# Log-softmax over rows of 50,000: two DMA queues and a register-counted loop over four 50 KB buffers

## The chip, the cores and the metric

The kernel runs on one NeuronCore of one Trainium2 chip. The metric is the device time of the whole program in microseconds (us). Before the change the median of 17 runs is 7909.7 us (7871.91 to 7929.28).

The names of the profile: PE is TensorE (matmul), PEld its weight load, DVE is VectorE, ACT is ScalarE, POOL is GpSimd and SP is SyncE, which here only issues transfers. "SPq" is SP's queue of instructions.

## The reference

The input has 16 x 512 = 8192 rows of 50,000 float32 numbers, 1638.4 MB. The output has the same shape. For each row:

```python
max_x = np.max(x, axis=-1, keepdims=True)
shifted = x - max_x
log_sum_exp = np.log(np.sum(np.exp(shifted), axis=-1, keepdims=True))
return (shifted - log_sum_exp).astype(np.float32)
```

Each number is read once and written once, so at least 3276.8 MB cross between HBM and the on-chip memory.

## The kernel before, in words

A row is cut into G = 8 pieces of 6,250 numbers, and each piece lies on its own partition. A tile has 16 rows, that is 128 partitions of 25,000 bytes, 3.2 MB; there are 512 tiles. Eight buffers hold tiles. Everything is unrolled in Python, and the order within each engine is the order in which the code is written (`manual_schedule`); engines wait for each other only through semaphores where data or buffers require it.

Three functions make up the work on a tile:

- `load(t)` issues the transfer of tile t on SP (L75).
- `front(t)`: VectorE takes the maximum of each partition (L81). A transpose (L84), a reduction over the 8 partitions of a row (L86), a copy that spreads the result (L91) and a second transpose (L96) give every partition the negative maximum of its row, `negmax`. ScalarE then takes the exponential of the tile in two pieces of 3,125, with the sum as a by-product in `part` (L102); the exponentials themselves go to a dump in PSUM and are not used. TensorE multiplies the two sums with a block matrix of ones, which adds them over the partitions of a row (L108), and ScalarE takes the logarithm (L112).
- `back(t)`: VectorE subtracts maximum and logarithm in place (L117), and SP issues the store of the tile (L121).

The main loop (L125 to L131) runs, for each t: load of tile t+5, front of tile t, back of tile t-1. So on VectorE the maximum of tile t is taken before tile t-1 is subtracted, and on SP loads and stores alternate in one queue. The load of tile t+5 goes into the buffer that tile t-3 had, so SP waits for the store of tile t-3 before it issues that load, and the store of tile t-1 stands behind it in SP's order.

Of the kernel before, what the change touches and what calls it, by code (L numbers as in the profile page):

```python
# [1 line left out]

# [4 lines left out]


FP32 = mybir.dt.float32
ACT = mybir.ActivationFunctionType  # L10
ALU = mybir.AluOpType
AX = mybir.AxisListType.X

P = 128
SQ = 32

G = 8
R = P // G
EXP_C = 3125
NBUF = 8  # L20
AHEAD = 5


@with_exitstack
def kernel(
    ctx: ExitStack,
    tc: tile.TileContext,
    x: bass.AP,
    out: bass.AP,
):  # L30
    nc = tc.nc
    xf = x.flatten_outer_dims()
    of = out.flatten_outer_dims()
    N, V = xf.shape
    W = V // G
    assert N % R == 0 and V % G == 0 and W % EXP_C == 0
    ntiles = N // R
    nexp = W // EXP_C

    xt = xf.rearrange("(t r) (g w) -> t (r g) w", r=R, g=G)  # L40
    ot = of.rearrange("(t r) (g w) -> t (r g) w", r=R, g=G)

    data = ctx.enter_context(tc.tile_pool(name="data", bufs=NBUF))
    stats = ctx.enter_context(tc.tile_pool(name="stats", bufs=4))
    consts = ctx.enter_context(tc.tile_pool(name="consts", bufs=1))
    dump_pool = ctx.enter_context(
        tc.tile_pool(name="dump", bufs=1, space=bass.MemoryType.PSUM)
    )
    sum_pool = ctx.enter_context(
        tc.tile_pool(name="sums", bufs=1, space=bass.MemoryType.PSUM)  # L50
    )

    ctx.enter_context(tc.manual_schedule())


    ones = consts.tile([P, P], FP32)
    nc.gpsimd.memset(ones, 1.0)  # L57
    ones3 = ones.rearrange("p (r g) -> p r g", g=G)
    nc.gpsimd.affine_select(  # L59
        out=ones3, in_=ones3, pattern=[[-G, R], [0, G]], base=0,  # L60
        channel_multiplier=1, compare_op=ALU.is_ge, fill=0.0,
    )
    nc.gpsimd.affine_select(  # L63
        out=ones3, in_=ones3, pattern=[[G, R], [0, G]], base=G - 1,
        channel_multiplier=-1, compare_op=ALU.is_ge, fill=0.0,
    )
    nc.scalar.preload_act_table_set("natural_log_exp_and_others")  # L67

    tiles = {}
    shift = {}  # L70
    logs = {}

    def load(t):
        buf = data.tile([P, W], FP32, name="buf")
        nc.sync.dma_start(out=buf, in_=xt[t])  # L75
        tiles[t] = buf

    def front(t):
        buf = tiles[t]
        pmax = stats.tile([P, 1], FP32, name="pmax")  # L80
        nc.vector.reduce_max(out=pmax, in_=buf, axis=AX)  # L81

        allmax = stats.tile([P, SQ], FP32, name="allmax")
        nc.vector.transpose(out=allmax, in_=pmax.to_broadcast([P, SQ]))  # L84
        rowmax = stats.tile([P, SQ // G], FP32, name="rowmax")
        nc.vector.tensor_reduce(  # L86
            out=rowmax, in_=allmax.rearrange("p (r g) -> p r g", g=G),
            op=ALU.max, axis=AX, negate=True,
        )
        spread = stats.tile([P, SQ], FP32, name="spread")  # L90
        nc.vector.tensor_copy(  # L91
            out=spread.rearrange("p (r g) -> p r g", g=G),
            in_=rowmax[:, :, None].to_broadcast([P, SQ // G, G]),
        )
        negmax = stats.tile([P, SQ], FP32, name="negmax")
        nc.vector.transpose(out=negmax, in_=spread)  # L96
        shift[t] = negmax

        part = stats.tile([P, nexp], FP32, name="part")
        for j in range(nexp):  # L100
            dump = dump_pool.tile([P, EXP_C], FP32, name="dump")
            nc.scalar.activation(  # L102
                out=dump, in_=buf[:, j * EXP_C : (j + 1) * EXP_C], func=ACT.Exp,
                bias=negmax[:, 0:1], scale=1.0, accum_out=part[:, j : j + 1],
            )
        rowsum = sum_pool.tile([P, 1], FP32, name="rowsum")
        for j in range(nexp):
            nc.tensor.matmul(  # L108
                rowsum, ones, part[:, j : j + 1], start=j == 0, stop=j == nexp - 1
            )  # L110
        logsum = stats.tile([P, 1], FP32, name="logsum")
        nc.scalar.activation(out=logsum, in_=rowsum, func=ACT.Ln)  # L112
        logs[t] = logsum

    def back(t):
        buf = tiles.pop(t)
        nc.vector.tensor_scalar(  # L117
            out=buf, in0=buf, scalar1=shift.pop(t)[:, 0:1], scalar2=logs.pop(t),
            op0=ALU.add, op1=ALU.subtract,
        )  # L120
        nc.sync.dma_start(out=ot[t], in_=buf)  # L121

    for t in range(AHEAD):
        load(t)
    for t in range(ntiles + 1):  # L125
        if t + AHEAD < ntiles:
            load(t + AHEAD)
        if t < ntiles:
            front(t)
        if t >= 1:  # L130
            back(t - 1)  # L131


# [1 line left out]
_INS = ['x']  # L135
_OUTS = [((16, 512, 50000), 'float32')]


# [23 lines left out]
```

## Time and profile before

| | |
|---|---|
| Median of 17 runs | 7909.7 us |
| Profiled execution | 7906.24 us |
| Its span, first to last instruction | 7904.5 us |
| VectorE busy | 5566.7 us (70%) |
| ScalarE busy | 3152.9 us (40%) |
| TensorE matmul busy | 600.3 us (8%) |
| HBM read / written | 1638.40 / 1638.40 MB, 415 GB/s over the span |
| Load, median from issue to landing | 23.6 us |
| Store, median from issue to landing | 30.7 us |

The page gives, for each group of instructions, the line of the code, the engine, what is written from what, the number of instructions, the busy time and the mean duration of one in ns, and after a second bar how long the engine stood idle just before them and what ended that. The row "GB/s" cuts the span into 40 equal slices. "DMA share" is the mean busy share of the 16 DMA engines. "The chain that ended last" is followed back from the last instruction, at each step to what released it.

### The profile page before, as it was taken

Reading aid. Unit: us, or ns where it says so; the run is one execution under the profiler, and the core shown is the slowest. Engines: PE = TensorE matmul, PEld = TensorE weight load, DVE = VectorE, ACT = ScalarE, POOL = GpSimd, SP = SyncE. Lnnn points to the kernel's source line nnn. Section 1 sums busy time; section 2 is a strip of 40 time slices with the busy share of each in tenths; the row PEclk is TensorE's granted clock in tenths of the full one; section 3 lists DMA queues with packets and bytes.
Section 4 is the critical chain, followed back from the end, with each engine's and each line's share of the span. In section 5 each row is a group of like instructions: output and inputs, shape, how many; then the busy total and the mean of one; then the engine's idle time right before and its main releaser. Section 6 shows DMA issues by size and latency. Waiting matters only on the chain.

```text
span 7904.5 us, 12333 instructions
## 1 busy us (share of the span) xinstructions
PE 600.3 (8%) x2048; PEld 512.9 (6%) x2048; DVE 5566.7 (70%) x3072; ACT 3152.9 (40%) x2561; POOL 1.2 (0%) x7
## 2 busy tenths in 40 slices
PE   0000000000000000000000000000000000000000
PEld 0000000000000000000000000000000000000000
DVE  8777777777777776766666666666676676767665
ACT  4444444444444444333343434343433434333333
POOL 0000000000000000000000000000000000000000
DMA  9999999999999999999999999999999999999999
GB/s 417 429 431 431 431 431 431 431 431 431 431 430 431 430 427 409 409 404 406 405 409 403 407 405 407 405 409 403 408 409 406 411 408 406 409 401 407 407 407 385
DMA packets 147536, 3277.65 MB, mean 415 GB/s; under 512 B 16384, under 2 KB 16384, under 8 KB 16384
## 3 DMA queue, kind: packets, MB, share of 16 engines
q1 hardware_dynamic: 147456, 3276.87, 99.9%
q14 instruction: 64, 0.52, 0.0%
q8 instruction: 16, 0.26, 0.0%
HBM read 1638.40 MB, written 1638.40 MB: 415 GB/s over the span
## 4 chain that ended last, share of the span: by engine, by line
DMA 97%; SPq 1%; DVE 1%; issue 0%; ACT 0%; PE 0%; ACTq 0%
DMA out_dram<-buf 97%; SPq L75 1%; DVE pmax L81 1%; DMA buf<-in_x_dram 0%; DVE buf L117 0%; ACT dump L102 0%; DVE allmax L84 0%; DVE rowmax L86 0%; DVE negmax L96 0%; DVE spread L91 0%; PE rowsum L108 0%; ACT logsum L112 0%; ACTq L102 0%
## 5 line engine op out<-in xcount | busy, mean ns | idle before, releaser
L81 DVE TENSOR_REDUCE pmax<-buf 128x1 f32<-128x6250 f32 x512 | 3411.7, 6663 | 2227.7 <-DMA buf<-in_x_dram 2227.7
L102 ACT ACTIVATE dump<-buf,negmax 128x3125 f32<-128x3125 f32 x1024 | 2938.0, 2869 | 4366.6 <-DVE negmax L96 4350.0
L117 DVE TENSOR_SCALAR buf<-buf,negmax,logsum 128x6250 f32<-128x6250 f32 x512 | 1789.7, 3496 | 4.5 <-ACT logsum L112 3.6
L108 PE MATMUL rowsum<-part,ones 128*128 128x1 f32 x2048 | 600.3, 362 | 7265.5 <-ACT dump L102 7265.5
L108 PEld LDWEIGHTS rowsum<-part,ones 128*128 128x128 f32 x2048 | 512.9, 311 | 7352.9 <-ACT dump L102 7331.3
L112 ACT ACTIVATE logsum<-rowsum 128x1 f32<-128x1 f32 x512 | 87.7, 171 | 345.8 <-PE rowsum L108 345.8
L102 ACT ACTIVATION_READ_ACCUMULATOR dump<-buf,negmax 128x1 f32 x1024 | 190.9, 186 | 0.0
L96 DVE STREAM_TRANSPOSE negmax<-spread 128x32 f32<-128x32 f32 x512 | 108.4, 212 | 17.7
L84 DVE STREAM_TRANSPOSE allmax<-pmax 128x32 f32<-128x32 f32 x512 | 108.3, 212 | 17.5
L86 DVE TENSOR_REDUCE rowmax<-allmax 128x4 f32<-128x32 f32 x512 | 95.2, 186 | 17.7
L91 DVE COPY spread<-rowmax 128x32 f32<-128x32 f32 x512 | 92.7, 181 | 17.8
L67 ACT ACT_TABLE_LOAD x1 | 1.3, 1283 | 0.8 <-PEq L146 0.8
L59 POOL TENSOR_SCALAR_AFFINE_SELECT ones<-ones 128x128 f32<-128x128 f32 x1 | 0.4, 405 | 0.1
L63 POOL TENSOR_SCALAR_AFFINE_SELECT ones<-ones 128x128 f32<-128x128 f32 x1 | 0.4, 399 | 0.1
L57 POOL MEMSET ones<- 128x128 f32 x1 | 0.2, 205 | 0.3 <-POOLq L146 0.3
L146 POOL MEMSET const-bfloat16-1.0<- 128x1 bf16 x1 | 0.1, 102 | 0.0
L146 POOL MEMSET const-uint8-127<- 128x1 uint8 x1 | 0.1, 102 | 0.0
L146 POOL MEMSET const-float32-0.0<- 128x1 f32 x1 | 0.1, 99 | 0.3 <-issue 0.3
L146 POOL MEMSET const-float32-1.0<- 128x1 f32 x1 | 0.1, 99 | 0.0
## 6 DMA issues: line engine op xcount, KB each, us to landing
buf<-in_x_dram SPq DMA_DIRECT2D x512, 3125.0 KB, 23.6
out_dram<-buf SPq DMA_DIRECT2D x512, 3125.0 KB, 30.7
```

Source lines behind the costliest of these rows:

```text
L59: nc.gpsimd.affine_select(out=ones3, in_=ones3, pattern=[[-G, R], [0, G]], base=0, channel_multiplier=1, compare_op=ALU.is_ge, fill=0.0,)
L67: nc.scalar.preload_act_table_set("natural_log_exp_and_others")
L75: nc.sync.dma_start(out=buf, in_=xt[t])
L81: nc.vector.reduce_max(out=pmax, in_=buf, axis=AX)
L84: nc.vector.transpose(out=allmax, in_=pmax.to_broadcast([P, SQ]))
L86: nc.vector.tensor_reduce(out=rowmax, in_=allmax.rearrange("p (r g) -> p r g", g=G), op=ALU.max, axis=AX, negate=True,)
L91: nc.vector.tensor_copy(out=spread.rearrange("p (r g) -> p r g", g=G), in_=rowmax[:, :, None].to_broadcast([P, SQ // G, G]),)
L96: nc.vector.transpose(out=negmax, in_=spread)
L102: nc.scalar.activation(out=dump, in_=buf[:, j * EXP_C : (j + 1) * EXP_C], func=ACT.Exp, bias=negmax[:, 0:1], scale=1.0, accum_out=part[:, ...
L108: nc.tensor.matmul(rowsum, ones, part[:, j : j + 1], start=j == 0, stop=j == nexp - 1)
L112: nc.scalar.activation(out=logsum, in_=rowsum, func=ACT.Ln)
L117: nc.vector.tensor_scalar(out=buf, in0=buf, scalar1=shift.pop(t)[:, 0:1], scalar2=logs.pop(t), op0=ALU.add, op1=ALU.subtract,)
```

## The change

A row now lies on G = 4 partitions, 12,500 numbers or 50,000 bytes on each. A tile has 32 rows and 6.4 MB, and there are 256 tiles. Four buffers of 50,000 bytes per partition are allocated once; the small tiles exist in two copies each.

The maximum is taken piece by piece: VectorE reduces a piece of 3,125 to its negative maximum, and ScalarE takes the exponential of that piece against this piece's own maximum. When all four pieces are done, the row's maximum is found from the four (one small reduction more, then transpose, reduction, copy and transpose as before), and ScalarE computes four factors exp(piece's maximum minus row's maximum), which VectorE multiplies with the four sums. TensorE adds them in four matmuls, and logarithm and subtraction follow. All of this is done for one tile before the next begins.

Stores are issued by ScalarE, loads by SP: the load of tile t+4 comes after the compute of tile t in the code. The first four tiles and the last four are written out; the 62 rounds between them are a loop on the chip, whose variable gives the DRAM addresses.

```diff
-G = 8
+G = 4
-NBUF = 8
-AHEAD = 5
+NBUF = 4
...
+    def load(j, t):
+        nc.sync.dma_start(out=bufs[j], in_=dram(xt, t))
...
+        for c in range(nexp):
+            piece = buf[:, c * EXP_C : (c + 1) * EXP_C]
+            nc.vector.tensor_reduce(
+                out=negm[:, c : c + 1], in_=piece, op=ALU.max, axis=AX, negate=True
+            )
+            nc.scalar.activation(
+                out=dump, in_=piece, func=ACT.Exp,
+                bias=negm[:, c : c + 1], scale=1.0, accum_out=part[:, c : c + 1],
+            )
+
+        nc.vector.tensor_reduce(out=negp, in_=negm, op=ALU.min, axis=AX)
+        nc.vector.transpose(out=allneg, in_=negp.to_broadcast([P, SQ]))
...
+        nc.vector.transpose(out=negmax, in_=spread)
+        nc.scalar.activation(
+            out=scale, in_=negm, func=ACT.Exp, bias=negmax[:, 0:1], scale=-1.0
+        )
+        nc.vector.tensor_mul(out=scaled, in0=scale, in1=part)
+        for c in range(nexp):
+            nc.tensor.matmul(
+                rowsum, ones, scaled[:, c : c + 1], start=c == 0, stop=c == nexp - 1
+            )
         nc.scalar.activation(out=logsum, in_=rowsum, func=ACT.Ln)
         nc.vector.tensor_scalar(
...
-        nc.sync.dma_start(out=ot[t], in_=buf)
+        nc.scalar.dma_start(out=dram(ot, t), in_=buf)
...
+    def round_of(t, last=False):
+        for j in range(NBUF):
+            compute(j, t + j)
+            if not last:
+                load(j, t + j + NBUF)
+
+    for j in range(NBUF):
+        load(j, j)
+    round_of(0)
+    with tc.For_i(NBUF, ntiles - NBUF, NBUF, iteration_sync="reg_based") as t:
+        with tc.manual_schedule():
+            round_of(t)
+    round_of(ntiles - NBUF, last=True)
```

## The prediction, made before the result was known

> **What bounds the kernel now.** I read the page from the top: engines, rate by slice, DMA queue, chain.
>
> ```profile
> PE 600.3 (8%) x2048; PEld 512.9 (6%) x2048; DVE 5566.7 (70%) x3072; ACT 3152.9 (40%) x2561; POOL 1.2 (0%) x7
> ...
> GB/s 417 429 431 431 431 431 431 431 431 431 431 430 431 430 427 409 409 404 406 405 409 403 407 405 407 405 409 403 408 409 406 411 408 406 409 401 407 407 407 385
> ...
> q1 hardware_dynamic: 147456, 3276.87, 99.9%
> ...
> DMA out_dram<-buf 97%; SPq L75 1%; DVE pmax L81 1%; DMA buf<-in_x_dram 0%; DVE buf L117 0%; ACT dump L102 0%; DVE allmax L84 0%; DVE rowmax L86 0%; DVE negmax L96 0%; DVE spread L91 0%; PE rowsum L108 0%; ACT logsum L112 0%; ACTq L102 0%
> ```
>
> No engine is above 70%; one queue keeps the 16 DMA engines busy throughout, and stores are 97% of the chain. The transfers are the bound: 3276.87 MB in 7904.5 us, 415 GB/s. But the rate has two levels, which stretches of the trace give exactly (third last column DMA share, last GB/s):
>
> ```profile
> 400.00:2800.00 2400.00, 188.89 (x645) 161.38 (x645) 1751.53 (x967) 991.86 (x808) 0.00 (x0) 1.00 1.00 431
> 3200.00:7600.00 4400.00, 328.33 (x1120) 280.51 (x1120) 3035.20 (x1675) 1721.62 (x1400) 0.00 (x0) 1.00 1.00 406
> ```
>
> At 431 throughout, the data would take 3276.87/0.431 = 7603 us; some 300 us go to the second level. The table of waits says who holds the next transfer back:
>
> ```profile
> DVE pmax L81 <- DMA buf<-in_x_dram: 2227.7, 503, 10.9
> ...
> SPq L75 <- DMA out_dram<-buf: 7331.1, 504, 23.9
> ```
>
> VectorE waits for loads, and SP, before each load, for the store that frees the buffer. The packet records under these views show more. A 25,000-byte packet takes 928 ns at the median in both stretches; of all packets, fewer than 1 in 100 exceed 1,000 ns between 800 and 2,400 us, and 12 in 100 after 3,200. Grouped by transfer, after 3,200 us a load takes a DMA engine about 8.1 us for its eight packets, a store 7.4; earlier both take 7.45. And the 16 parts of one transfer land 0.55 us apart at the start, 6 us apart at 760 us, 11.3 at 2,240 and 12 to 14 from 2,840 on: one engine is some 0.5% slower, the others run ahead of it until they have no descriptor left. At 2,811 us a load lands on the leading engine 10.3 us after its issue, hardly more than the 10.0 of the very first load, which found an empty queue. From there on the leaders wait for each new load, bunch together (14 of 16 within 3 us), all load at once and then all store at once. Why loads are slow in that state the trace does not say; that it begins there, it does.
>
> **What the Trainium skill says.** "DMA: Bandwidth & Descriptors", Issuing engines are not separate DMA queues: transfers from SP and ScalarE share the same 16 engines, so two issuers add no bandwidth. Same page, Queues, rings and completion order: each engine goes round-robin between rows that have work, packet by packet. Before has one data queue, so its trace can show neither. Same page, Specifications: the fabric's ceiling is 435 GB/s; the trace's 431 agrees. "Runtime: NRT & Kernel Launch", Instruction fetch mechanics: a taken branch whose target is out of the instruction window stalls for a fetch; no loop here shows it.
>
> **The change part by part.** The group rows that price it:
>
> ```profile
> L81 DVE TENSOR_REDUCE pmax<-buf 128x1 f32<-128x6250 f32 x512 | 3411.7, 6663 | 2227.7 <-DMA buf<-in_x_dram 2227.7
> L102 ACT ACTIVATE dump<-buf,negmax 128x3125 f32<-128x3125 f32 x1024 | 2938.0, 2869 | 4366.6 <-DVE negmax L96 4350.0
> L117 DVE TENSOR_SCALAR buf<-buf,negmax,logsum 128x6250 f32<-128x6250 f32 x512 | 1789.7, 3496 | 4.5 <-ACT logsum L112 3.6
> ...
> L112 ACT ACTIVATE logsum<-rowsum 128x1 f32<-128x1 f32 x512 | 87.7, 171 | 345.8 <-PE rowsum L108 345.8
> L102 ACT ACTIVATION_READ_ACCUMULATOR dump<-buf,negmax 128x1 f32 x1024 | 190.9, 186 | 0.0
> ...
> L86 DVE TENSOR_REDUCE rowmax<-allmax 128x4 f32<-128x32 f32 x512 | 95.2, 186 | 17.7
> L91 DVE COPY spread<-rowmax 128x32 f32<-128x32 f32 x512 | 92.7, 181 | 17.8
> ```
>
> *Transfers.* The bytes stay; 1,024 transfers of 3.2 MB become 512 of 6.4 MB. At 431 GB/s a load takes 14.85 us and load plus store 29.7; 256 tiles take 7603. This is gained only if reads and writes stay mixed, as between 400 and 2,800 us.
>
> *Compute of one tile.* It is now serial: the old front of tile t+1 before back of tile t is gone. Reductions: L86 and L81 give (6663-186)/(6250-32) = 1.042 ns an element, so 3,125 take 3.41 us, four 13.6. Each exponential (2.87+0.19) runs under the next reduction; the last stands out, 3.1. The small minimum, transpose, reduce, copy and transpose, 5 x 0.2 = 1.0, hide under it. Then the exp of four scales 0.17 (as L112), product 0.18 (as L91), hops 0.3. One matmul to its logarithm took 0.67 before; three more at 0.5 make 2.2. Logarithm 0.17. The subtraction: (3496-181)/6218 = 0.533 ns an element, 6.8 for 12,500. Sum 26.5, say 27, against 29.7 of transfer: hidden, with 2.7 us to spare. Uncovered, everything over 29.7 would cost 256 times itself.
>
> *Store issued by ScalarE.* 0.46 us each (as on SP). The new wait there is for the tile's subtraction; behind it on ScalarE stand the next tile's exponentials, and the first of these needs a reduction that VectorE ends 3.4 us after the subtraction. Nothing is late; without that cover it would be 256 x 0.46 = 118 us.
>
> *Load issued after compute.* SP has only loads left and still waits for the store of the same buffer. A buffer's round is load 29.7 (shared), compute 27, store 29.7 and two times about 2.6 us of latency (first load: 10.0 to landing less 7.4 of data): 92 against 4 x 29.7 = 119 available. The 27 to spare become a queue of stores, so on every engine a store nearly always waits beside a load; that covers the lag of the slow engine too.
>
> *Loop.* Branches, register waits and addresses are in no row of before. Lower bound nothing; hidden as long as a round of four tiles takes compute under 119, that is up to 119-108 = 11 us a round. Upper bound: engines join and drain (rival below). I take nothing.
>
> *Ends.* First bytes after 2.6 us; last store 3. With two stores still queued when the last load lands (30 us of transfer against 27 of compute), the tail has no hole. The slow engine's own 0.5% is 38.
>
> Sum of the span: 7603+38+3+3 = 7647, against 7904.5. The profiled execution took 1.7 more than its span and the median of the runs 3.5 more than that: 7650.
>
> **Rivals.** (1) Two rings do not restore 431: either each switch of ring costs something, or loads that begin as they are issued are slow as in the second stretch. For it: with four buffers mostly one load is outstanding. Against: stores are always beside it. At 407 throughout: 3276.87/0.407 = 8051+45 = 8096, slower than before; a mixture gives about 7900. It decides from 417.5 GB/s down (3276.87/(7894-45)).
>
> (2) The serial tile becomes the bound. Chain 27 plus register waits at every hop; it decides from 30.7 us a tile (7849/256). At 31.2: 7990+45 = 8035. Against: it takes 3.7 us more than rows add up to.
>
> (3) The back edge joins all engines and drains transfers. Then each round ends with a store and a load of 14.9+2.6 each behind 108 of compute: 143 us, 64 rounds are 9150. It decides at 14 us a round beyond the 108. Against: the code names a synchronisation by registers for the loop and writes no barrier; for it: the trace of before has no loop to look at.
>
> (4) Nothing changes, because the two-level rate belongs to the addresses: 7900. Against: the onset falls where the leaders run dry.
>
> **How the numbers follow.** Forecast 0.56 (its own range 7580 to 7730); rival 1 0.22, of which 0.05 still faster and 0.02 the same; rival 2 0.09; rival 3 0.10; rival 4 0.03, half of it the same. Faster 0.61, same 0.04, slower 0.35, where 0.2% is about what a measurement of this kernel can tell from no change. 7570 to 8110 leaves out rival 3 and small ends of the others. If packets of 50,000 bytes saved their fixed part, 0.5%, it would lie inside.
>
> **What would show it.** Right: two data queues with 50/50 bytes; GB/s at 428 to 433 in nearly all slices; VectorE waits 2 to 3 us a tile for a load; SP waits on stores for most of the span. Wrong: a rate near 407 with DMA share 1.00 (rival 1); VectorE without waits for loads, DMA share below 0.98 (2); holes every 120 us or more on all engines (3); a step at some 2,840 us again (4).

## The result, and the profile after

The changed kernel takes 9863.78 us (median of 8 runs, 9852.83 to 9873.81); its ratio to the kernel before is 1.2482 (95% interval 1.2464 to 1.2501). The forecast was 7650, with a range of 7570 to 8110. So the direction and the range were wrong.

The page of the changed kernel, rate by slice, DMA queues, and median time from issue to landing:

```profile
DMA  9998989899899898898988989898888998989986
GB/s 389 340 334 329 334 330 337 332 332 336 327 335 332 331 335 327 332 334 328 336 328 333 337 329 337 328 336 332 331 331 328 337 334 330 333 326 335 335 325 276
...
q1 hardware_dynamic: 36864, 1638.42, 46.5%
q10 hardware_dynamic: 36864, 1638.42, 43.0%
...
buf<-in_x_dram SPq DMA_DIRECT2D x256, 6250.0 KB, 38.3
out_dram<-buf ACTq DMA_DIRECT2D x256, 6250.0 KB, 38.4
```

Two queues carry half of the bytes each, as forecast. But the rate is 332 GB/s almost from the start, lower than either level of before, and the DMA engines are no longer busy throughout (46.5% and 43.0% make 89.5). So something holds transfers back. The table of waits says what:

```profile
ACT dump L101 <- DMA out_dram<-buf: 4349.6, 183, 24.8
DVE scaled L122 <- ACT scale L119: 3677.0, 256, 16.2
...
ACT dump L101 <- issue: 1475.8, 61, 25.1
...
DVE negm L98 <- DMA buf<-in_x_dram: 19.0, 1, 19.0
```

VectorE waited for a load once, at the start; loads are on time. Before, it had waited for them 2227.7 us. What is new is the first line: ScalarE's exponentials, which read a loaded tile, are released by a *store* (the 61 under "issue" stand behind a store as well). The timeline of one tile shows why this is so (start, duration, engine, line; lines of small operations left out):

```profile
3994.79 6.79 DVE L128 TENSOR_SCALAR buf<-buf,negmax,logsum 128x12500 f32<-128x12500 f32 x1 [2.23 <-ACT logsum L127]
...
4017.61 0.36 ACTq L132 DMA_DIRECT2D out_dram<-buf  x1
4018.22 2.87 ACT L101 ACTIVATE dump<-buf,negm 128x3125 f32<-128x3125 f32 x1 [23.46 <-DMA out_dram<-buf]
...
4032.94 6.79 DVE L128 TENSOR_SCALAR buf<-buf,negmax,logsum 128x12500 f32<-128x12500 f32 x1 [2.22 <-ACT logsum L127]
...
4056.59 0.33 SPq L88 DMA_DIRECT2D buf<-in_x_dram  x1
4056.60 0.36 ACTq L132 DMA_DIRECT2D out_dram<-buf  x1
```

The subtraction ends at 4001.58, but its store is issued 16 us later, at 4017.61. The next subtraction ends at 4039.73, its store goes at 4056.60, and 0.01 us before it SP issues a load, which waits for the store of the tile before. Two instructions on two engines that start together point to the same event: the landing of the previous store. From store to store it is 39.0 us here, and a store takes 38.4 from issue to landing. Exactly one store, and with it one load, is under way at any time.

The built program confirms the wait. In the loop, each store carries, beside the wait for its subtraction, one for the semaphore that the store before it raises (the store of buffer 0, not listed, waits for all four stores of the round before); the stores in the written-out first round carry none:

```
first round: store of buffer 1    waits: VectorE (subtraction)
loop:        store of buffer 1    waits: VectorE (subtraction), DMA semaphore 0 (raised by the store of buffer 0)
             store of buffer 2    waits: VectorE (subtraction), DMA semaphore 2 (raised by the store of buffer 1)
             store of buffer 3    waits: VectorE (subtraction), DMA semaphore 4 (raised by the store of buffer 2)
```

In the loop a store's place in the output is known only when the loop runs. Two stores to one tensor with unknown places are kept in order, as if they could overlap; the run with independent stores, below, takes this away and nothing else.

The cost per tile (6.4 MB in and 6.4 MB out), worked out from packet records: the base is the packets of one DMA engine at the shortest usual duration (after: eight of a load and eight of a store at 1,847 ns; before: twice as many at 928 ns), "slow" what they take beyond it, "hole" the time in which the engine moves nothing.

| Stretch | us per 12.8 MB | base | slow packets | hole | GB/s |
|---|---|---|---|---|---|
| before, 400 to 2,800 us | 29.7 | 29.7 | 0.1 | 0 | 431 |
| before, 3,200 to 7,600 us | 31.5 | 29.7 | 1.7 | 0.1 | 406 |
| after, 1,000 to 9,000 us | 38.55 | 29.55 | 5.1 | 3.9 | 332 |

So the wait costs twice: 3.9 us in which an engine has nothing to move, and 5.1 us because packets take longer on average (loads 2,254 ns and stores 2,079, instead of 1,847). The slowing is uneven. Half of the load packets still take 1,847 ns; the first load packet of each engine after the halt takes 3,485 ns on average, which alone makes 1.6 of the 5.1 us.

### The profile page after: what moved, and what is told of

It is laid out like the page before. It is cut to its first block, busy times and chain, and to the rows that moved or that the text cites. A ratio compares the mean times of both kernels' runs of the same rounds, so it can differ in the third digit from the quotient of the medians.

```text
span 9863.2 us, 18331 instructions
## 1 busy us (share of the span) xinstructions
PE 476.0 (5%) x2048; PEld 455.9 (5%) x2048; DVE 5417.5 (55%) x2816; ACT 3156.4 (32%) x2561; POOL 1.4 (0%) x7
## 3 DMA queue, kind: packets, MB, share of 16 engines
q1 hardware_dynamic: 36864, 1638.42, 46.5%
## 5 line engine op out<-in xcount | busy, mean ns | idle before, releaser
L101 ACT ACTIVATE dump<-buf,negm 128x3125 f32<-128x3125 f32 x1024 | 2936.9, 2868 | 6116.4 <-DMA out_dram<-buf 4349.6
L98 DVE TENSOR_REDUCE negm<-buf 128x1 f32<-128x3125 f32 x1024 | 3416.6, 3399 | 141.6 <-PEq L173 73.5
L128 DVE TENSOR_SCALAR buf<-buf,negmax,logsum 128x12500 f32<-128x12500 f32 x256 | 1738.4, 6791 | 561.4 <-ACT logsum L127 561.4
L124 PE MATMUL rowsum<-scaled,ones 128*128 128x1 f32 x2048 | 476.0, 354 | 9363.0 <-DVE scaled L122 9363.0
L124 PEld LDWEIGHTS rowsum<-scaled,ones 128*128 128x128 f32 x2048 | 455.9, 328 | 9383.1 <-DVE scaled L122 7010.6
L101 ACT ACTIVATION_READ_ACCUMULATOR dump<-buf,negm 128x1 f32 x1024 | 190.7, 186 | 0.0
L119 ACT ACTIVATE scale<-negm,negmax 128x4 f32<-128x4 f32 x256 | 72.1, 282 | 0.0
L116 DVE STREAM_TRANSPOSE negmax<-spread 128x32 f32<-128x32 f32 x256 | 54.2, 212 | 13.3
L107 DVE STREAM_TRANSPOSE allneg<-negp 128x32 f32<-128x32 f32 x256 | 54.2, 212 | 8.9
L108 DVE TENSOR_REDUCE rowneg<-allneg 128x8 f32<-128x32 f32 x256 | 47.6, 186 | 8.9
## 6 DMA issues: line engine op xcount, KB each, us to landing
buf<-in_x_dram SPq DMA_DIRECT2D x256, 6250.0 KB, 38.3
out_dram<-buf ACTq DMA_DIRECT2D x256, 6250.0 KB, 38.4
```

The lines of the kernel that those rows point to most:

```text
L98: nc.vector.tensor_reduce(out=negm[:, c : c + 1], in_=piece, op=ALU.max, axis=AX, negate=True)
L101: nc.scalar.activation(out=dump, in_=piece, func=ACT.Exp, bias=negm[:, c : c + 1], scale=1.0, accum_out=part[:, c : c + 1],)
L107: nc.vector.transpose(out=allneg, in_=negp.to_broadcast([P, SQ]))
L108: nc.vector.tensor_reduce(out=rowneg, in_=allneg.rearrange("p (r g) -> p r g", g=G), op=ALU.min, axis=AX,)
L119: nc.scalar.activation(out=scale, in_=negm, func=ACT.Exp, bias=negmax[:, 0:1], scale=-1.0)
L124: nc.tensor.matmul(rowsum, ones, scaled[:, c : c + 1], start=c == 0, stop=c == nexp - 1)
```

## The experiments

A store or load is called outstanding from its issue to its landing. Theory A: the time is lost because each store of the loop waits for the store before it. Rivals: B, two queues with 6.4 MB transfers are slow in themselves; C, the serial compute or the loop's own instructions are the bound.

**Written out.** The 62 rounds are a Python loop, everything else as in the changed kernel.

```diff
-    with tc.For_i(NBUF, ntiles - NBUF, NBUF, iteration_sync="reg_based") as t:
-        with tc.manual_schedule():
-            round_of(t)
+    for t in range(NBUF, ntiles - NBUF, NBUF):
+        round_of(t)
```

> The changed kernel with its 62 rounds written out instead of looped, so that every store has a fixed address and none waits for the store before it; all else is as in the changed kernel. Theory A (in the loop each store waits until the store of the tile before has landed, because the loop's addresses are not known to differ): the wait is gone, the round of a tile falls from 38.8 us to the transfers, 29.6 us at the rate of 1847 ns a 50,000-byte packet, and the time to 7600 to 7700. Theory B (two queues with 6.4 MB transfers are slow by themselves, as packets of 2250 and 2080 ns in the changed kernel say): 34.6 us a tile, about 8900. Theory C (serial compute or its waits are the bound): over 9500, as now.

Measured: 7667.13 us, ratio to before 0.9707 (0.9627 to 0.9788), as A expects. The four runs, 7615.06, 7617.08, 7717.18 and 7823.15 us, scatter more than those of any other kernel here; why, no trace shows. The profiled execution is the one of 7615.06; its rates and waits:

```profile
GB/s 417 433 433 431 434 435 433 433 434 434 434 433 434 433 434 433 433 432 432 434 433 431 433 433 433 433 430 432 431 430 432 432 426 430 432 430 431 433 431 379
```

```profile
DVE negm L98 <- DMA buf<-in_x_dram: 998.4, 252, 18.6
```

The same 6.4 MB transfers on the same two queues run at 430 to 435 GB/s in nearly all slices, with packets of 1,859 ns (loads) and 1,848 (stores) on average; B is out. VectorE waits for every load, 3.9 us a tile: the transfers are the bound and the serial compute is covered, so that half of C is out. The other half, the loop's own instructions, left together with the wait; the next two runs separate them.

**Loop with independent stores.** The loop stays; its stores are declared independent.

```diff
...
+            for i, s in enumerate(mine):      # mine: the four stores of the body
+                for k, r in enumerate(mine):
+                    if k < i:
+                        tc.declare_no_dep(s, r, reason=...)
+                    tc.declare_no_dep(s, r, across_iterations=True, reason=...)
```

> The loop stays, but its stores are declared independent of each other, so each waits only for its own subtraction and for its own buffer's store one round before. Theory A: the same time as the written-out kernel within 1%, plus some 60 us for draining at the loop's entry. If the loop itself costs time (branches, register waits): more than that, by the same amount in each round.

Measured: 7681.54 us (7677.32 to 7689.59), ratio 0.9729 (0.9703 to 0.9755). One removed wait gives back what the change had lost:

```profile
GB/s 400 406 433 433 432 434 433 434 433 433 433 434 433 434 434 433 434 433 433 433 430 432 434 434 433 434 434 433 434 434 433 432 430 432 429 431 432 433 433 256
```

The loop's branches and register waits cost nothing that shows, and the fetch stall that the prediction named for a branch doesn't show either: from 1,000 to 7,000 us 12.8 MB take 29.57 us, in the written-out kernel 29.63. At the loop's entry (SPq) and exit (PEq) the engines do drain, once each:

```profile
DVE negm L98 <- DMA buf<-in_x_dram: 927.7, 240, 19.0
...
DVE negm L98 <- PEq L180: 70.8, 1, 70.8
DVE negm L98 <- SPq L145: 48.2, 1, 48.2
```

Part of this is covered: the span of this profiled execution is 62 us longer than the written-out kernel's, about the 60 expected.

**Written out, wait put back by hand.** The rounds are a Python loop again.

```diff
...
+        s = nc.scalar.dma_start(out=dram(ot, t), in_=buf)
+        if stores and NBUF < t < ntiles - NBUF:
+            tc.add_manual_dep(s, stores[-1].name, <data dependency>)
+        stores.append(s)
```

> The rounds are written out, and the wait is put back by hand: each store waits until the store of the tile before has landed. No loop, no register waits. Theory A: 9800 to 9900, the time of the changed kernel. If the loop as such is what costs, it stays near the written-out kernel.

Measured: 9742.46 us (two runs, 9740.11 and 9744.82), ratio 1.2335 (1.2292 to 1.2377); 1.2% less than the changed kernel and just below the expected range. About half of these 121 us is a shorter time per tile (38.3 instead of 38.55 us, 248 times); the rest is about what the drains at the loop's ends had cost above. The wait alone, without any loop, makes the loss: 38.3 us per 12.8 MB, of which 5.0 slow packets and 3.7 hole. ScalarE stands behind stores again:

```profile
ACT dump L101 <- DMA out_dram<-buf: 5854.5, 246, 31.5
```

**Stores on SP, loop kept.** One word: `nc.scalar.dma_start` becomes `nc.sync.dma_start` for the store.

> The changed kernel with its stores issued by SP instead of ScalarE; the loop stays. SP's own order now holds the stores apart: after a store comes the load of its buffer, which waits for that store to land, and the next store stands behind it. ScalarE is never blocked. If what costs in the changed kernel is ScalarE standing still before the next tile's exponentials, this one falls to 7700 or below. If it is that only one store is ever outstanding (theory A), it stays far above: between 8700 (29.6 us of transfer plus a hole of 4 us a tile, packets at full speed) and 9860.

Measured: 8784.76 us, ratio 1.1114 (1.1079 to 1.1149), inside the range expected of theory A. ScalarE no longer waits for a store at all (no such line in the table of waits), and still about half of the loss remains (1,118 of the 2,197 us over the written-out kernel). SP's queue shows the same pairing, load and store issued together every 34 us:

```profile
4006.24 0.34 SPq L88 DMA_DIRECT2D buf<-in_x_dram  x1
4007.29 0.35 SPq L132 DMA_DIRECT2D out_dram<-buf  x1
4040.96 0.34 SPq L88 DMA_DIRECT2D buf<-in_x_dram  x1
4041.52 0.35 SPq L132 DMA_DIRECT2D out_dram<-buf  x1
```

So a blocked ScalarE doesn't explain the loss. In the changed kernel it wasn't on the path either: the subtraction was done 16 us before its store could go. What counts is that one store at a time may be outstanding. In one queue the load goes first and the store after it, packets are less slowed and the halt is shorter: 34.07 us = 29.55 + 1.9 slow + 2.6 hole. This edit changes two things at once, a free ScalarE and a single queue; no run separates which of them gave back the other half.

**Two back instead of one.** The wait by hand, but on `stores[-2]`.

> The written-out kernel with each store waiting for the store two tiles before, not for the one just before. Theory A: two stores may be outstanding, so the wait is nearly always over when it is asked (a store lands some 48 us after its issue in the written-out kernel, a tile takes 30): 7620 to 7900. If any wait of a store on a store costs as much as in the chained kernel, about 9700.

Measured: 7631.67 us (7617.0 and 7646.33), ratio 0.9655 (0.9603 to 0.9707). With two stores allowed the wait costs nothing. The step between free and 2,100 us is one outstanding store, here with two queues and 6.4 MB tiles.

**Two queues in the kernel before.** One word in the other direction: L121 on `nc.scalar`.

> The kernel before with one edit: stores are issued by ScalarE instead of SP; tiles, buffers and order stay. If two queues keep loads and stores mixed on each DMA engine, the second level of the rate (406 GB/s after 2,840 us) does not come, and the time is 7600 to 7700. If two queues cost something by themselves (theory B), it is above 8000. If the level belongs to addresses, nothing changes: 7900.

Measured: 7614.07 us (7613.99 to 7614.22), ratio 0.9640 (0.9615 to 0.9666). The second level of the rate is gone:

```profile
GB/s 425 433 432 432 432 432 432 432 432 432 432 432 432 432 432 432 432 432 432 432 432 432 432 432 432 432 432 432 432 432 432 431 433 432 431 433 432 431 433 380
```

The Trainium skill ("DMA: Bandwidth & Descriptors", Issuing engines are not separate DMA queues) says a second issuer adds no bandwidth. The trace agrees on the packet, 928 ns with one queue and with two; the 3.6% come from packets that are no longer slowed. Its suggestion to give loads and stores an issuing engine each, for "more dynamic spread" ("Perfetto Trace Analysis", DMA Optimizations), is what this run does, though the page makes it above all for loops and this kernel has none.

**Why before has two levels.** Three runs on one queue change which store a load waits for.

> The kernel before with seven buffers instead of eight and loads four tiles ahead instead of five, one queue. If the second level of the rate begins where the leading DMA engines run out of descriptors, one tile less in flight brings it to the start of the run: about 406 GB/s throughout, 8070 to 8150, no step at 2,840 us. If the step belongs to addresses or to time, it stays where it is: 7900.

> The kernel before with one number changed: loads four tiles ahead instead of five, eight buffers, one queue. The load before which SP waits then needs the buffer of a store one tile older, so one tile more of transfers (14.85 us) may be queued. The seven-buffer run could not tell, because there the distance between load and awaited store had stayed at eight less three. If the second level begins where the leading engines run out of descriptors, the lag they may build up grows from 12 to about 27 us; at the 0.42% by which they lead, the step moves from 2,840 to some 6,500 us, and the time falls to about 7700. If it belongs to addresses or time: step at 2,840 us, 7900.

> The kernel before with loads six tiles ahead instead of five: one tile less of transfers may be queued, so there is no lag to build up. If the second level begins where the leaders run dry, it is there from the first 100 us on: 406 GB/s or less throughout, 8050 or more. If it belongs to addresses or time: 7900 with the step at 2,840 us.

Seven buffers, four ahead: 7896.59 us, ratio 0.9971 (0.9943 to 0.9999), the step still there. The expected 8070 to 8150 did not come, but this run was badly chosen and can't decide. Load t+4 with seven buffers waits for the store of tile t-3, just as load t+5 with eight does; the number of tiles in flight in SP's queue had not changed. The next two runs move that distance. Four ahead with eight buffers (load waits for the store of t-4): 7670.42 us, ratio 0.9715 (0.9675 to 0.9755), near the expected 7700. Six ahead (t-2): 9721.65, ratio 1.2313 (1.2266 to 1.2360), right in sign, but far above the expected 8050. Their rates, four ahead first:

```profile
GB/s 414 425 429 430 430 431 431 431 431 430 431 431 431 431 431 431 431 431 431 431 431 431 431 431 431 431 431 431 431 430 430 430 431 430 430 421 419 410 413 362
```

```profile
GB/s 356 338 334 334 338 335 335 338 337 341 338 337 334 336 336 334 336 337 341 338 340 336 337 336 334 336 333 341 337 338 333 336 332 335 334 334 336 336 337 356
```

With one tile more in the queue the step moves from 2,840 to some 6,700 us (6,500 expected); with one less the rate is low from the start, and deeper: 336 GB/s, with DMA engines busy only 88% of the time, where they were busy throughout on the second level of before. Bytes and addresses are the same in all three, so the step belongs to the depth of the queue. Six ahead is the more telling run: it has no loop, one queue, small tiles, and loses nearly what the changed kernel loses. Its SP holds the next store behind a load which waits for the store before, so one store at a time is outstanding (in before it is two, with loads four ahead three). Per 12.8 MB it takes 38.1 us = 29.7 + 3.7 slow + 4.7 hole. "One store at a time" can come from a wait on the store itself or from the place of another instruction's wait in a queue.

**Serial stores with small tiles.** Before on two queues (as above), with each store waiting for the one before.

> The kernel before with stores on ScalarE, and each store waiting until the store of the tile before has landed: 512 serial stores of 3.2 MB instead of 256 of 6.4 MB. Per tile 14.85 us of transfer at 928 ns a packet, the hole of 4.1 us a store that the changed kernel shows, and its slow packets. If their excess (5.1 us a tile of 6.4 MB) grows with the bytes, 2.6 us: 21.5 us, 11,000. If it belongs to each restart, 5.1 us: 24 us, 12,300. If eight buffers keep loads running in the hole, below 9500.

Measured: 9367.95 us, ratio 1.1852 (1.1817 to 1.1886). I had expected 11,000 or more, or below 9500 if loads fill the hole. The time falls below 9500, but not for that reason: the DMA engines are busy only 88% of the time. Transfers halt twice per 12.8 MB, but each halt is shorter, 2.2 us instead of 3.9, and slow packets fall to 1.3 a tile: 36.7 us = 29.7 + 2.6 slow + 4.4 hole. Of the 1.3, the first load packet of each engine makes 1.0 (1,975 instead of 928 ns). Neither part is a constant per restart; why they are smaller here stays open.

**The two halves without the loop.** Loads after the store in the code and seven tiles ahead, stores on ScalarE, small tiles; then the same with the changed kernel's large tiles and four buffers, three ahead.

```diff
+            back(t - 1)
+        if t + AHEAD < ntiles:
+            load(t + AHEAD)
```

> The kernel before with stores on ScalarE, and loads issued after the store in the code and seven tiles ahead: the first half of the change alone, without larger tiles and without loop. The transfers at 928 ns a packet set the time: 7603 and some 11 for the ends, 7614, as with loads five ahead. If depth of prefetch matters beyond the second queue, it is lower.

> As the run before, but with the changed kernel's tiles: a row on 4 partitions, four buffers of 50,000 bytes per partition, loads three ahead, everything written out, and the old order of work (maximum of tile t before the subtraction of tile t-1). Packets of 50,000 bytes take 1847 ns and not 2 x 928, 0.5% less, so 7565 and some 45 for longer ends: about 7610, at best a tie. If one tile in the wrong place with four buffers starves the loads, 7700 or more.

Seven ahead: 7614.12 us, ratio 0.9644 (0.9620 to 0.9667), equal to five ahead; these two are the fastest kernels of the study. Large tiles in the old order of work: 7978.2 us, ratio 1.0098 (1.0066 to 1.0130), about 1% slower than before. The tie did not come; it is the other branch, 7700 or more. Its timeline shows how late a store goes:

```profile
4002.22 6.75 DVE L117 TENSOR_SCALAR buf<-buf,negmax,logsum 128x12500 f32<-128x12500 f32 x1
...
4015.13 0.17 ACT L112 ACTIVATE logsum<-rowsum 128x1 f32<-128x1 f32 x1 [0.68 <-PE rowsum L108]
4015.19 0.34 ACTq L121 DMA_DIRECT2D out_dram<-buf  x1
```

A tile is subtracted only after the next tile's maximum has been taken, and its store then stands on ScalarE behind the next tile's exponentials and logarithm: it goes at 4015.19, 6.2 us after its subtraction. As I read it, of four buffers two are held by compute and little more than one load and one store is left in transfer (each some 33 us to landing, against 44.3 and 48.1 in the written-out changed kernel). So the changed kernel's serial order, which I had counted as a price, seems to be what makes four buffers suffice. The two kernels also differ in how far ahead loads run and in the maximum by pieces, and no run takes these apart.

## Why the prediction was wrong, point by point

*The bound and the base* were right. The transfers set the time, 12.8 MB take 29.6 us when enough are queued, and the kernel that the prediction described, two queues with several stores waiting, takes 7667.13 us written out (7615 to 7823) and 7681.54 looped, against 7650 forecast. The 0.5% that larger packets could save is real (1,847 instead of 2 x 928 ns).

*The compute of one tile*: 27 us forecast. In the changed kernel's written-out first round one tile follows the other at 25.7 us (reductions at 44.77 and 70.45 us). Right, and covered: written out, VectorE waits 3.9 us a tile for loads.

*"Store issued by ScalarE ... Nothing is late"* failed. The step counted the wait for the subtraction and nothing else. In the loop the store has a second wait, for the store before, and that one came 16 us after the first. The exponentials queued behind it were late too, but off the path: the next subtraction was still done 16 us before its store could go, and the run with stores on SP, which frees them, stays at 8784.76 us.

*"Loop. Lower bound nothing ... I take nothing"* is the step that decided. I had priced branches, register waits and a barrier. Branches and register waits cost nothing, as taken; the drain exists only once at entry (49.0 us of VectorE waiting) and once at exit (73.5). The price was in none of these: in this loop the stores' addresses are unknown when the program is built, so stores that the written-out code knows to be apart become ordered, and a tile takes 38.55 us instead of 29.6. What was in the diff to see was `dram(ot, t)` with a loop variable as the destination of every store.

*"The 27 to spare become a queue of stores"* shows how much hung on it. The round of a buffer was right, but the spare time was to sit in a queue of two stores, and the loop allows one. With the steps' own terms: 38.55 instead of 29.6 us over some 250 tiles is 2240 us; the profiled spans of the changed and the written-out kernel differ by 2250.

*The rivals.* Rival 1 had two halves. That a switch between queues costs something is out: two queues run at 432 GB/s. That loads which begin as they are issued are slow did come (2,254 ns a packet), as 5.1 of the 9.0 us lost per tile, and its argument, that mostly one load is outstanding, was the right warning; but it foresaw 407 GB/s with engines busy throughout, not 332 with halts, and named no cause in the loop. Rival 2 did not occur. Rival 3 came nearest in time (9150) but has the wrong mechanism: there is no joining at the back edge, and the holes come with each tile, not each round. Rival 4, that the two levels belong to addresses, is refuted by the runs four and six ahead and by the second queue.

*The two levels of before*: the reading that the onset lies where the leading DMA engines run out of descriptors held, as it put the step of the run four ahead at 6,500 us, and 6,700 was measured. What remains open is why packets slow down then. In the kernels of this study packets slow down in the stretches in which DMA engines wait for each new transfer, most of all the first load packet after a halt, and hardly in those with a standing queue; that is a coincidence shown, not a mechanism. No run separated it further.

## What to carry to other kernels

When a loop on the chip replaces written-out code, list for each transfer what it must wait for when its address is not known, above all stores to one tensor; a single wait of each store on the one before turned a kernel 3% faster into one 25% slower, and declaring the stores independent gave it all back. In a kernel bound by transfers, ask how many loads and stores may be outstanding between one landing and the next issue. On two queues two stores cost nothing here and one cost 2,100 us. Where the order of a single queue set the number it was 9722 us with one, about 7900 with two and 7670 with three, against 7614 on two queues. And give loads and stores an issuing engine each, so that a load waiting for its buffer doesn't hold up a store that is ready: one word in the kernel before, 3.6%.

## What the runs showed of the hardware that was not expected

Packets of the same size and on the same queues take 1,847 ns with a standing queue, and on average 2,254 (loads) and 2,079 (stores) when every store and load is issued on the landing of the last; the slowing is larger than the idle time itself (5.1 against 3.9 us a tile). A third of it sits in the first load packet of each engine after the halt, 3,485 ns. With 25,000-byte packets, two queues and serial stores it is loads that suffer, 1,076 against 943 ns on average, and among them mainly the first, 1,975.

With two queues the 16 parts of a store or load drift apart without harm: in the kernel before on two queues the spread of the 16 landings grows from 2 us to some 20 us in one half of the transfers and 30 in the other by 7,200 us, far over the 12 us at which the one-queue kernel fell to its second level, and the rate stays at 432 GB/s.
